# The state and diagonal products of one unit in four move a pair later, beside the transposes of the unit that follows a pair of B and C

## The chip, the cores and the metric

The kernel runs on one core of one Trainium2 chip. The metric is the device time of one execution in microseconds (us), as the median of three runs, 1308.15 us before the change (1307.92 to 1314.77). TensorE (PE) multiplies, VectorE (DVE) and ScalarE (ACT) work on what it leaves in PSUM, GpSimd (POOL) and SyncE (SP) issue transfers between HBM and SBUF.

## The reference

One layer of a Mamba-2 mixer over 512 positions and 2048 channels, with an RMSNorm ahead and one behind. Cut to what matters here:

```python
hn = rmsnorm(x, ln_g)                      # 512 x 2048
z, xbc, dt = split(hn @ w_in)              # 4096 | 4096 + 8*128 (B) + 8*128 (C) | 64
xbc = silu(causal_depthwise_conv(xbc, conv_w, conv_b))       # 4 taps
xs, B, C = split(xbc)                      # 64 heads of 64 channels, 8 groups of B and C
# per head, in chunks, with decay exp(cumsum(A*dt)) between positions:
y_diag = (C B^T * decay) @ (xs * dt)       # inside a chunk
y_off  = (C @ state) * exp(cs)             # what the state of earlier chunks brings
y = (y_diag + y_off + d_skip * xs) * silu(z)
out = rmsnorm(x + rmsnorm(y, norm_g) @ w_out, final_g)
```

## The kernel before, in words

All matrices are split into a rounded part (hi) and a remainder (lo); a product of two such pairs is three matmuls of 128x128 by 128x256. ACT writes hi (L87), DVE subtracts to get lo (L88). The channels of x and z are cut into 32 **units** of 128 channels (two heads each), the groups of B and C into 8 pairs of tiles. The order of the work is a list: B0 C0, then x and z of units 0 and 1, then B1 C1, unit 2, 3, 4, 5, then B2 C2, unit 6, 7, 8, 9, then B3 C3, and so on: a **pair of B and C** stands between units 4g+1 and 4g+2. The first four entries are computed plainly (the ramp, steps 0 to 127). Each later entry (`pair`, 36 of them) takes its two tiles together by a scheme of seven products (`product`, L629) in place of eight, called R11, T1, R22, T2, R21, T3 and T4; their weights are sums of pieces of `w_in` that are loaded, added and split.

**Steps.** A pair is 28 steps (QS) of six matmuls each, a plain tile 16. Everything that isn't a product of the projection is an event at a step (`add`, `run`): before the matmuls of a step PE, SP and POOL issue the events of that step. The orders of PE, SP and POOL are written by hand in this way; on DVE and ACT a scheduler sets the order when the program is built, with what stands under `urgent` preferred. All queues are in order, so an instruction that waits holds what is behind it.

**A unit's own work.** After product T3 of its pair, DVE adds the parts of x (L687 reads the PSUM tile `R`, L691 the tile `S`, both write the tile `xr`), scales them (L693) and runs the convolution (`conv_silu`, L388 and three times L391), and ACT applies SiLU (L394, tile `xs`). z follows a few steps later (`gate`, L643 and L644). Then, at steps counted from the unit's own start, in the table `steps` (six numbers: load, decay, transposes, state, diagonal product, end):

- load, 42: SP loads the tile `csb` (L440) and `ecs` (L443).
- decay, 54 (`u_decay`): twelve ACT instructions of 128x128 (L456, L457, L458), one exponential (L459) and a multiply on DVE (L461) fill the tile `m`. `m`, like `csb`, `xd` and `xw`, has one buffer.
- transposes, 44 (`u_xt`, L473): PE transposes `xs`, DVE makes `xd` (L476) and `xw` (L479).
- state, 72 (`u_state`, L488): PE multiplies `Bt` and `xw`; ACT and DVE split the result (L403, L404).
- diagonal product, 72 (`u_yd`, L502, L506): PE multiplies `xd` and `m`; DVE adds it to `xs` (L509).
- end, 78 (`u_yo`, L518 to L520): C times the state; DVE L521 to L523 form the result `z`, SP writes it to HBM (L524, `yscr`), ACT and DVE sum its squares (L529, L530).

With 28 steps between units, step 72 of one unit is step 44 of the next: the state and diagonal products of unit u stand right ahead of the transposes of unit u+1. Where a pair of B and C stands between, they are apart: unit 5 has its state and diagonal products in unit 6's pair, and the transposes of unit 6 stand alone in unit 7's pair, 28 steps later.

**The ramp.** Units 0, 1 and 31 have rows of their own. At steps 114 to 126 `x_form3` (L575 to L579) rewrites parts of the input through `xr`, one after the other. The last plain tile, C1, is scaled into `xr` (L398) and convolved from there before the first pair may write `xr` at L687.

**The end of the pairs.** The output projection's first weight pieces are loaded by `get_out`: piece 0 into `rc` nine steps, piece 1 into `rb` four steps before the last pair ends. `rb` has one buffer.

## Time and profile before

| | |
|---|---|
| median of three runs | 1308.15 us (1307.92 to 1314.77) |
| the profiled execution's own time | 1305.56 us |
| its span, first to last instruction | 1303.8 us |
| mean granted clock of PE | 0.985 |
| busy share PE, DVE, ACT | 95%, 83%, 65% |
| busy of GpSimd | 77.8 us (6%) |
| moved by DMA | 225.90 MB, mean 173 GB/s |

The span is the time from the first to the last instruction; the run's own time lies 1.8 us above it. Busy time of PE counts pipelined matmuls and is no measure of its peak. A row of a timeline reads: start, length, engine, line, operation, output tile <- input tiles, and in brackets how long the engine was idle before it and what ended that. A row of the waits reads: engine, tile and line that waited, what for, total us, times, longest. A row of the windows reads: stretch, its length, busy us of each engine (instructions), the granted clock as a fraction of full speed, the DMA share.

### The profile page before, as it was taken

The page shows a single profiled execution, that of the slowest core. Times are in us where ns is not written, and L with a number is a line of the kernel's source. Part 1 is how long each engine was busy: PE and PEld are TensorE (multiplying, and loading weights), DVE is VectorE, ACT ScalarE, POOL GpSimd, SP SyncE. Part 2 cuts the span into 40 slices and gives each one's busy share as a digit, 9 for nine tenths or more (in the row PEclk, how much of TensorE's full clock was granted, in tenths as well). Part 3 has the DMA queues.
Part 4 walks back from the last instruction along what each step waited for, and adds up shares of the span by engine and source line. Part 5 has one row for each costly group of instructions (what it writes and reads, how often), then busy time and mean ns, then how long its engine had stood idle before and what let it go on. Part 6 is the DMA issues. An engine that isn't in the chain of part 4 may idle for free.

```text
span 1303.8 us, 24525 instructions
## 1 busy us (share of the span) xinstructions
PE 1243.5 (95%) x9932; PEld 1185.1 (91%) x9932; DVE 1081.8 (83%) x1449; ACT 847.0 (65%) x1371; POOL 77.8 (6%) x99
## 2 busy tenths in 40 slices
PE   8989899989989999999999999999999999999897
PEld 8979799989989998998999899899978899899885
DVE  5796889978989998898989789898856987877765
ACT  7667677667768767776786777678666445434433
POOL 0000000000000000000000000010000000000000
PEclk9999999999999999999999999999999999999999
DMA  9546756666667667667675666666437676657612
GB/s 358 184 132 175 182 149 163 177 162 193 164 164 191 160 170 171 194 153 190 177 179 154 183 168 163 190 169 184 138 105 230 190 198 204 189 125 217 184 57 97
DMA packets 70194, 225.90 MB, mean 173 GB/s; under 512 B 8384, under 2 KB 12800, under 8 KB 69952
## 3 DMA queue, kind: packets, MB, share of 16 engines
q1 hardware_dynamic: 56688, 176.34, 38.6%
q0 software_dynamic: 12672, 46.14, 22.4%
q8 instruction: 78, 1.28, 0.4%
q10 hardware_dynamic: 720, 1.84, 0.4%
q14 instruction: 36, 0.29, 0.1%
HBM read 211.52 MB, written 12.78 MB: 172 GB/s over the span
## 4 chain that ended last, share of the span: by engine, by line
PE 59%; DVE 16%; DMA 11%; ACT 7%; issue 6%; SPq 0%; DVEq 0%; ACTq 0%
PE S L636 4%; PE S L638 4%; PE S L637 4%; PE R L636 4%; PE R L637 4%; PE R L638 4%; DMA csb<-cscr 3%; DVE lo L88 3%; PE mm L636 3%; PE mm L637 3%; PE mm L638 3%; PE mm L932 3%; PE mm L934 3%; PE mm L933 3%; ACT hi L87 3%
## 5 line engine op out<-in xcount | busy, mean ns | idle before, releaser
L88 DVE TENSOR_TENSOR lo<-ra,hi 128x1024 fp32r<-128x1024 f32 x150 | 183.3, 1222 | 48.2 <-ACT hi L87 48.0
L87 ACT CAST hi<-ra 128x1024 fp32r<-128x1024 f32 x150 | 157.0, 1049 | 95.8 <-PE S L637 30.0
L636 PE MATMUL R<-s,hi 128*128 128x256 f32 x576 | 166.9, 290 | 2.3 <-DVE xr L687 2.3
L638 PE MATMUL R<-s,lo 128*128 128x256 f32 x576 | 162.4, 282 | 0.9 <-DVE lo L88 0.9
L637 PE MATMUL R<-s,hi 128*128 128x256 f32 x576 | 162.5, 282 | 0.0
L638 PE MATMUL mm<-xh,lo 128*128 128x256 f32 x576 | 159.4, 277 | 1.5 <-DVE lo L88 1.5
L636 PE MATMUL mm<-xh,hi 128*128 128x256 f32 x576 | 159.3, 277 | 0.0
L637 PE MATMUL mm<-xl,hi 128*128 128x256 f32 x576 | 159.2, 276 | 0.0
L87 ACT CAST hi<-rc 128x1024 fp32r<-128x1024 f32 x94 | 99.0, 1054 | 89.8 <-PE R L637 36.0
L88 DVE TENSOR_TENSOR lo<-rc,hi 128x1024 fp32r<-128x1024 f32 x94 | 115.1, 1225 | 35.2 <-ACT hi L87 35.0
L636 PEld LDWEIGHTS R<-s,hi 128*128 128x128 f32 x576 | 111.9, 194 | 3.6 <-DVE xr L687 2.5
L638 PEld LDWEIGHTS R<-s,lo 128*128 128x128 f32 x576 | 111.4, 193 | 1.1 <-DVE lo L88 1.1
L637 PEld LDWEIGHTS R<-s,hi 128*128 128x128 f32 x576 | 111.7, 194 | 0.0
L638 PEld LDWEIGHTS mm<-xh,lo 128*128 128x128 f32 x576 | 108.3, 188 | 1.9 <-DVE lo L88 1.9
L636 PEld LDWEIGHTS mm<-xh,hi 128*128 128x128 f32 x576 | 108.1, 188 | 0.3 <-issue 0.2
L637 PEld LDWEIGHTS mm<-xl,hi 128*128 128x128 f32 x576 | 108.1, 188 | 0.0
L605 DVE TENSOR_TENSOR ra<-ra,rc 128x1024 f32<-128x1024 f32 x88 | 107.5, 1222 | 0.4
L636 PE MATMUL S<-xh,h1h 128*128 128x256 f32 x288 | 79.7, 277 | 0.0
L638 PE MATMUL S<-s,lo 128*128 128x256 f32 x288 | 79.7, 277 | 0.0
L637 PE MATMUL S<-xl,h1h 128*128 128x256 f32 x288 | 79.6, 277 | 0.0
L638 PE MATMUL S<-xh,h1l 128*128 128x256 f32 x288 | 79.6, 277 | 0.0
L636 PE MATMUL S<-s,hi 128*128 128x256 f32 x288 | 79.6, 276 | 0.0
(448 smaller groups left out, 3958.1 us busy)
## 6 DMA issues: line engine op xcount, KB each, us to landing
rc<-in_wi SPq DMA_DIRECT2D x76, 512.0 KB, 5.1
ra<-in_wi SPq DMA_DIRECT2D x42, 512.0 KB, 6.0
rb<-in_wi SPq DMA_DIRECT2D x40, 512.0 KB, 4.6
ra<-in_wi POOLq DMA_DIRECT2D x36, 512.0 KB, 6.2
rb<-in_wi POOLq DMA_DIRECT2D x36, 512.0 KB, 6.2
csb<-cscr SPq DMA_DIRECT2D x32, 512.0 KB, 5.4
ra<-in_wo SPq DMA_DIRECT2D x26, 512.0 KB, 5.2
yscr<-z SPq DMA_DIRECT2D x32, 256.0 KB, 4.4
```

The costliest lines, as they stand in the source:

```text
L87: S.copy(out=hi, in_=raw)
L88: V.tensor_tensor(out=lo, in0=raw, in1=hi, op=ALU.subtract)
L605: V.tensor_tensor(out=raw, in0=raw, in1=qs[n][other], op=ALU.add)
L636: T.matmul(ps, hi[:, k, :], ah, start=first and k == 0, stop=False, skip_group_check=True)
L637: T.matmul(ps, hi[:, k, :], al, start=False, stop=False, skip_group_check=True)
L638: T.matmul(ps, lo[:, k, :], ah, start=False, stop=k == KH - 1, skip_group_check=True)
L932: T.matmul(ps, yh, hi, start=first and k == 0, stop=False)
L933: T.matmul(ps, yh, lo, start=False, stop=False)
L934: T.matmul(ps, yl, hi, start=False, stop=last and k == 1)
```

## The change

Three things are changed. In the table, units 5, 9, 13, 17, 21 and 25 (the units ahead of a pair of B and C) have state and diagonal product at step 100 in place of 72 and the end at 106 in place of 78: one pair later, in the same step as the transposes of the next unit and ahead of them. Units 0 and 1 get the same pattern: state and diagonal product of unit 0 stand ahead of unit 1's transposes (step 136 of the whole), those of unit 1 ahead of unit 2's (step 172). In the first pair the sum of x is formed in place in the tile `sn`, which holds the copies, and only the scaling (L693) writes `xr`. And the load of the second output piece is issued three steps earlier than its split.

```diff
+    def out_load(n, name):
+        oraw[n] = load_piece(wo_src(*wo_order[n]), OSH, name)
...
     def get_out(n, name="ra"):
         if n < len(wo_order) and n not in opieces:
-            opieces[n] = split_piece(load_piece(wo_src(*wo_order[n]), OSH, name), OSH,
+            raw = oraw.pop(n) if n in oraw else load_piece(wo_src(*wo_order[n]), OSH, name)
+            opieces[n] = split_piece(raw, OSH,
                                      *((op, ("oh", "ol")) if n % 4 == 3 else (wp,)))
...
         sn = sp.tile([P, 2, LH], F32, name="sn")
-        zq = xr[:, 3:L + 3]
+        zq = sn.rearrange("p h l -> p (h l)") if n == 0 else xr[:, 3:L + 3]
...
-        V.scalar_tensor_tensor(out=zq, in0=zq, scalar=-1.0, in1=rbc, op0=ALU.mult, op1=ALU.mult)
+        V.scalar_tensor_tensor(out=xr[:, 3:L + 3], in0=zq, scalar=-1.0, in1=rbc, op0=ALU.mult, op1=ALU.mult)
...
-    steps = {0: [66, 71, 63, 75, 87, 92], 1: [56, 65, 50, 68, 86, 92], NU - 1: [36, 46, 44, 65, 65, 71]}
+    steps = {0: [66, 71, 63, 104, 104, 114], 1: [56, 76, 72, 108, 108, 114], NU - 1: [36, 46, 44, 65, 65, 71]}
+    for u in range(5, NU - 4, UPG):
+        steps[u] = [42, 54, 44, 100, 100, 106]
...
-    add(END - 4, get_out, 1, "rb")
+    add(END - 7, out_load, 1, "rb")
+    add(END - 4, get_out, 1)
```

How this moves instructions is read from the order of the built program. Line numbers of the changed file are 6 higher from L165 to L716 (L394 becomes L400) and 8 or 9 higher behind that.

ACT, from unit 6's pair into unit 7's, before: `m<-csb` is unit 6's decay, `xs<-xs` its SiLU.

```order
L87 CAST h1h<-ra 128x1024
L660 COPY mm<-S 128x256
L456 ACTIVATE m<-csb,cs 128x128
L457 ACTIVATE m<-csb,cs 128x128
L458 ACT_TABLE_LOAD
L458 ACTIVATE m<-csb,nwl 128x128
L665 COPY sn<-R 128x256
L87 CAST hi<-rc 128x1024
L456 ACTIVATE m<-csb,cs 128x128
L394 ACT_TABLE_LOAD
L394 ACTIVATE xs<-xs 128x512
L644 ACTIVATE z<-z 128x512
```

The same place after the change; `stsh` is now the split of unit 5's state:

```order
L87 CAST h1h<-ra 128x1024
L666 COPY mm<-S 128x256
L87 CAST hi<-rc 128x1024
L671 COPY sn<-R 128x256
L400 ACTIVATE xs<-xs 128x512
L87 CAST hi<-rc 128x1024
L650 ACTIVATE z<-z 128x512
L87 CAST hi<-rb 128x1024
L688 COPY sn<-S 128x256
L409 CAST stsh<-yo 128x128
L462 ACTIVATE m<-csb,cs 128x128
```

The decay moved from ahead of the SiLU to behind it, and a table load went. `m` is read by the diagonal product of unit 5, which now stands in this pair too.

SP, in the pairs of units 6 and 7, before: `yscr` is unit 5's result, the `csb` and `ecs` behind it are unit 6's.

```order
L81 DMA rc<-in_wi 128x1024
L81 DMA rb<-in_wi 128x1024
L524 DMA yscr_101<-z 128x512
L440 DMA csb<-cscr 128x1024
L443 DMA ecs<-escr 64x256 x2
L81 DMA rc<-in_wi 128x1024
L81 DMA ra<-in_wi 128x1024
L81 DMA rc<-in_wi 128x1024
L81 DMA rb<-in_wi 128x1024
L440 DMA csb<-cscr 128x1024
```

After:

```order
L81 DMA rc<-in_wi 128x1024
L81 DMA rb<-in_wi 128x1024
L446 DMA csb<-cscr 128x1024
L449 DMA ecs<-escr 64x256 x2
L81 DMA rc<-in_wi 128x1024
L81 DMA ra<-in_wi 128x1024
L81 DMA rc<-in_wi 128x1024
L81 DMA rb<-in_wi 128x1024
L530 DMA yscr_101<-z 128x512
L446 DMA csb<-cscr 128x1024
```

The write of unit 5's result moved from ahead of unit 6's `csb` to ahead of unit 7's.

DVE, in the first pair and the one behind it, before: L687 and L691 form the first pair's sum, `bc` is the convolution of C1.

```order
L398 TENSOR_TENSOR xr<-S,rbc 128x512
L88 TENSOR_TENSOR lo<-ra,hi 128x1024
L388 TENSOR_SCALAR bc<-xr,par 128x512
L605 TENSOR_TENSOR ra<-ra,rc 128x1024
L391 SCALAR_TENSOR_TENSOR bc<-xr,par,bc 128x512
L521 TENSOR_TENSOR ecs<-yo,ecs 128x256
L391 SCALAR_TENSOR_TENSOR bc<-xr,par,bc 128x512
L522 TENSOR_TENSOR xs<-xs,ecs 128x256
L391 SCALAR_TENSOR_TENSOR bc<-xr,par,bc 128x512
L523 TENSOR_TENSOR z<-xs,z 128x512
L687 TENSOR_TENSOR xr<-R,sn 128x256
L691 TENSOR_TENSOR xr<-S,sn 128x256
```

After; `m` is unit 1's, `lo<-rb` the split of the first pair's T3, L583 and L585 belong to the last `x_form3`:

```order
L467 TENSOR_TENSOR m<-m,cbm 128x1536
L693 TENSOR_TENSOR sn<-R,sn 128x256
L582 TENSOR_TENSOR xr<-xr,xl 128x512
L88 TENSOR_TENSOR lo<-rb,hi 128x1024
L583 TENSOR_TENSOR xr<-xr,xl 128x512
L529 TENSOR_TENSOR z<-xs,z 128x512
L88 TENSOR_TENSOR lo<-ra,hi 128x1024
L585 TENSOR_TENSOR xl<-xr,xh 128x2x256
L88 TENSOR_TENSOR lo<-ra,hi 128x1024
L697 TENSOR_TENSOR sn<-S,sn 128x256
L404 TENSOR_TENSOR xr<-S,rbc 128x512
```

The first pair's sum moved from behind C1's convolution to ahead of C1's scaling (L398, now L404), and the split of T3 and the last `x_form3` now stand behind its first half.

## Prediction

> **What bounds the kernel now.** First the head of the page and its chain, then the waits of PE:

> ```profile
> span 1303.8 us, 24525 instructions
> PE 1243.5 (95%) x9932; PEld 1185.1 (91%) x9932; DVE 1081.8 (83%) x1449; ACT 847.0 (65%) x1371; POOL 77.8 (6%) x99
> PE 59%; DVE 16%; DMA 11%; ACT 7%; issue 6%; SPq 0%; DVEq 0%; ACTq 0%
> ```

> ```profile
> PE tr L473 <- ACT xs L394: 22.4, 7, 4.4
> PE mm L932 <- DVE z L643: 2.8, 1, 2.8
> PE R L636 <- DVE xr L687: 2.3, 1, 2.3
> PE mm L638 <- DVE lo L88: 1.5, 2, 1.2
> PE R L638 <- DVE lo L88: 0.9, 1, 0.9
> ```

> PE is the bound, and time is to be had only where it waits or its clock is lowered. The largest wait comes seven times: the transposes (L473) wait for a SiLU (L394). There are 32 units; the seven are units 2, 6, 10, 14, 18, 22 and 26, those behind a pair of B and C. The timelines of DVE, SP, ACT and PE at unit 6 show why:

> ```profile
> 259.96 0.69 DVE L523 TENSOR_TENSOR z<-xs,z 128x512 f32<-128x512 f32 x1
> 260.68 0.33 SPq L524 DMA_DIRECT2D yscr<-z  x1
> 261.05 0.46 SPq L440 DMA_DIRECT2D csb<-cscr  x1
> 266.75 1.54 DVE L391 SCALAR_TENSOR_TENSOR xs<-xr,par,xs 128x512 f32<-128x512 f32 x2
> 268.95 0.41 ACT L456 ACTIVATE m<-csb,cs 128x128 f32<-128x128 f32 x1 [5.38 <-DMA csb<-cscr]
> 272.89 1.28 ACT L394 ACT_TABLE_LOAD   x1
> 274.18 0.63 ACT L394 ACTIVATE xs<-xs 128x512 f32<-128x512 f32 x1
> 274.86 1.12 PE L473 MATMUL tr<-ident,xs 128*128 128x128 f32 x4 [4.38 <-ACT xs L394]
> ```

> The convolution is done at 268.29, but the SiLU starts only at 274.18: ahead of it in ACT's queue stands the decay's first instruction, which waits for `csb` until 268.95; `csb` was held on SP behind unit 5's `yscr`, which waited for `z`. In an ordinary pair the decay can't be put there, because `m` has one buffer and the preceding unit's diagonal product reads it in the same step. The windows of six periods (five pairs each, from one unit's end to that of the fourth after) give the price; the first, the last and the sum of the six:

> ```profile
> core 0: us, PE busy (x) PEld busy (x) DVE busy (x) ACT busy (x) POOL busy (x), PEclk, DMA share, GB/s
> 188.21:303.03 114.82, 110.44 (x960) 107.81 (x959) 99.61 (x128) 81.95 (x139) 8.60 (x10) 0.99 0.64 170
> 753.60:865.20 111.60, 108.40 (x960) 105.78 (x959) 99.51 (x128) 81.53 (x138) 8.57 (x10) 1.00 0.65 174
> sum 676.99, PE 657.20 PEld 641.47 DVE 597.32 ACT 490.61 POOL 51.63; mean PE 109.53 PEld 106.91 DVE 99.55 ACT 81.77 POOL 8.60
> ```

> PE idles 676.99 - 657.20 = 19.8 us in them. The same 960 instructions take 108.40 us busy in the last, at clock 1.00, and 110.44 in the first, at 0.99 in the mean: 657.20 - 6 x 108.40 = 6.8 us more.

> **The change part by part.**

> *Units 5 to 25.* No instruction of PE or DVE is added. The state and diagonal products go into the next unit's pair, ahead of the transposes that waited. Three things follow. First, the decay of unit 6 must now wait until unit 5's diagonal product has read `m`, so ACT has it behind the SiLU, as in ordinary pairs. Second, `csb` loses its place behind `yscr` on SP; `yscr` now stands ahead of unit 7's `csb`, where an ordinary pair has it. Third, DVE's work on unit 5 (L404, L509, L521 to L523, L530) leaves a stretch in which DVE had no idle time and enters one where it idled. Three stretches show that cover, an ordinary pair, the one that ends unit 5's work, and the stretch with unit 7's pair behind the wait:

> ```profile
> 211.64:233.52 21.88, 21.88 (x197) 21.30 (x196) 20.03 (x26) 18.02 (x32) 1.71 (x2) 1.00 0.70 186
> 233.52:255.02 21.50, 21.50 (x193) 20.92 (x192) 21.29 (x28) 13.51 (x24) 1.74 (x2) 1.00 0.60 155
> 276.00:303.03 27.03, 27.03 (x228) 26.45 (x228) 22.39 (x27) 21.38 (x38) 1.72 (x2) 0.97 0.70 200
> ```

> DVE was busy 21.29 of 21.50 us in the second and 22.39 of 27.03 in the third. The ordinary pair runs its 21.88 us without any PE wait with DVE busy 20.03, and unit 7's pair becomes such a pair. PE reached the transposes at 274.86 - 4.38 = 270.48; the SiLU can start once the convolution ends at 268.29 at the latest and takes 0.63, so it is done by 269 with nothing ahead of it, and the products moved in front give PE more work before it asks. I take the whole 19.8 + 6.8 = **26.6 us**. From below: if DVE, at 99.5 of 108.4 us, puts back 1 us per period, 20.6. More than 26.6 there is not, since 108.40 is PE's own work.

> The second part of that sum is the clock. Windows right behind a wait: two in the ramp, one at unit 10, one at the end:

> ```profile
> 147.61:151.30 3.69, 3.69 (x19) 3.69 (x20) 3.69 (x6) 1.95 (x5) 0.19 (x1) 0.56 0.86 218
> 161.50:165.20 3.70, 3.70 (x21) 3.70 (x20) 0.77 (x2) 2.35 (x6) 0.00 (x0) 0.54 0.61 214
> 388.70:392.40 3.70, 3.70 (x33) 3.70 (x34) 2.26 (x3) 3.68 (x6) 0.00 (x0) 1.00 0.78 281
> 947.17:951.00 3.83, 3.83 (x11) 3.08 (x12) 1.08 (x1) 2.17 (x5) 0.00 (x0) 0.61 0.96 278
> ```

> Behind most waits, that of 2.3 us included (at 147.61), PE is granted little more than half its clock for about 3.5 us and does 19 to 21 matmuls where 33 fit. [...]

> *The ramp.* Four waits can go: 2.3 (L687), the first unit's share of the seven, 22.4 - 19.8 = 2.6, and 1.2 and 0.9 for splits. Behind the first two lie the clock windows at 147.61 and 161.50; 3.7 us at a clock of 0.55 lose about 1.6 each. Together 7.0 + 3.2 = 10.2. The first pair's wait goes since its sum no longer stands behind C1's convolution:

> ```profile
> 145.86 0.75 DVE L391 SCALAR_TENSOR_TENSOR bc<-xr,par,bc 128x512 f32<-128x512 f32 x1
> 147.13 0.43 DVE L687 TENSOR_TENSOR xr<-R,sn 128x256 f32<-128x256 f32 x1
> 147.46 0.42 DVE L691 TENSOR_TENSOR xr<-S,sn 128x256 f32<-128x256 f32 x1
> 140.55 0.69 DVE L398 TENSOR_TENSOR xr<-S,rbc 128x512 f32<-128x512 f32 x1
> ```

> New waits come in. The second pair's R11 takes the PSUM buffer of C1, which is free only after L398, and that now stands behind L691, which waits for the end of T3: PE waits 0.42 + 0.69, about 1.2 us with the handover. T3's own lo split stands behind unit 1's decay multiply, L687 and an `x_form3` row, and the last `x_form3`, which T3 reads, behind more splits; splits of 1024 columns take 1.23 (L88, below) and rows of 512 columns 0.69 (L398), so two or three rows too late are 1 to 2.5 us, an estimate. Unit 2's transposes may wait about 1 us, its last tap (L391) being behind the split of unit 1's state. That takes back some 3 to 5 of 10.2. I take **5 us** net; ends 10.2 (no new wait) and -2 (7 us of new waits, and the clock lowered behind three of them at 1.6 each).

> *The output piece.* At the end of the pairs:

> ```profile
> 929.74 1.22 DVE L88 TENSOR_TENSOR lo<-rb,hi 128x1024 fp32r<-128x1024 f32 x1
> 936.86 0.37 SPq L81 DMA_DIRECT2D rb<-in_wo  x1
> 942.75 1.05 ACT L87 CAST hi<-rb 128x1024 fp32r<-128x1024 f32 x1 [3.36 <-DMA rb<-in_wo]
> 943.84 1.23 DVE L88 TENSOR_TENSOR lo<-rb,hi 128x1024 fp32r<-128x1024 f32 x1 [1.73 <-ACT hi L87]
> 946.43 0.68 DVE L643 TENSOR_TENSOR z<-mm,rbc 128x512 f32<-128x512 f32 x1
> 947.17 0.80 PE L932 MATMUL mm<-hi,h1h 128*128 128x512 f32 x1 [2.82 <-DVE z L643]
> ```

> The load was issued at 936.86 behind `yscr`; moved ahead of it, it needs only `rb`, free when L88 ends at 930.96, so it lands some 5.9 us earlier (942.75 - 936.86 = 5.9 from issue), near 937. DVE's 1.73 of waiting goes, and the split, now ahead of the convolution, costs what it cost. So L643 comes 1.7 earlier, and PE's 2.82 shrinks to 1.1; with a smaller wait the low clock behind it (0.61 over 3.83 us, 1.5 us) goes: **3.2 us**. Ends: 1.5 (the clock stays low) and 4.3 (no wait is left).

> Sum: 26.6 + 5 + 3.2 = 34.8. The profiled execution took 1305.56, so 1270.8; the median of the three runs lies 2.6 above it, so **1273**.

> **The rivals.**

> *A new bound in the period.* DVE is at 92% of 108.4, and DMA would move the same bytes in less time. If waits for splits fill half of what is freed, 26.6 becomes 13, the ramp 2 and the end 2: 1291. For it: DVE's 21.29 of 21.50 in the pair of B and C. Against it: the ordinary pairs run at 20.03 of 21.88 without a wait, with a DMA share of 0.70.

> *Slower: T3's split ahead of unit 5's state.* In unit 7's pair ACT now has `hi<-rb` (the weights of T3, whose sum GpSimd fetches) ahead of `sn<-S` and `stsh`; if that transfer is late, the copy, the state, the decay and the SiLU's successors all wait, at six places. GpSimd's row of that transfer and the split before:

> ```profile
> 259.80 0.86 POOL L599 DMA_DIRECT2D rb<-in_wi  x1 [14.18 <-DMA rb<-in_wi]
> 276.73 1.05 ACT L87 CAST hi<-rb 128x1024 fp32r<-128x1024 f32 x1
> rb<-in_wi POOLq DMA_DIRECT2D x36, 512.0 KB, 6.2
> ```

> It lands near 259.80 + 6.2 = 266.0, before PE's 270.48. It makes the kernel slower by 0.5% when it costs (34.8 + 6.5) / 6 = 7 us at each place, that is, from a landing at 277.5: 1315. Eleven us of delay have no source in the trace.

> *The change doesn't do what it says.* If the SiLU has another late input, the seven waits stay, and the end alone gains: about 1305. Against it: 268.29 is the last input's time.

> **How the numbers follow.** About 0.5%, 6.5 us, is what a measurement can tell from no change. The forecast has 0.80 (its own range 1267 to 1281: 41.1 with every term at its upper end, 20.6 + 5 + 1.5 = 27.1 with the first and the last at their lower), the new bound 0.12 (1282 to 1296), no change 0.04, slower 0.04. For 8 in 10 the range goes from 1267 to 1287, into the second case. Faster 0.92, within 0.5% 0.04, slower 0.04.

> **What would show it.** In the changed profile PE's wait for `xs` (L400) is gone or under 2 us in all; each period of four units takes 108.4 to 109.5 us at clock 1.00; ACT no longer waits for `csb` in the periods; PE starts the ramp's L473 of unit 2 without a low clock behind it, and has instead a wait of about 1.2 us of `S` for `xr` (L404); PE's wait for L649 near the end is under 1 us. The prediction is wrong if the periods stay above 110.5, or if PE waits for `lo` (L88) several us in them.

## The result, and the profile after

The changed kernel takes 1274.83 us (median of six runs, 1270.53 to 1279.47) where the kernel before, timed beside it, takes 1308.88 (1307.92 to 1314.77). The ratio is 0.9728 with a 95% interval of 0.9700 to 0.9757, that is, 35.6 us less (31.8 to 39.3); the ratio is worked out from all the runs, the two medians lie 34.05 apart. The forecast was 1273, from a sum of 34.8.

In the changed kernel the line numbers around the units' work are 6 higher: the transposes are L479, the SiLU is L400, the decay L462 to L464, the gate of z L649. The head of its page, and one of PE's waits:

```profile
span 1272.2 us, 24491 instructions
PE 1233.7 (97%) x9932; PEld 1176.2 (92%) x9932; DVE 1079.9 (85%) x1449; ACT 827.5 (65%) x1357; POOL 77.5 (6%) x99
```

```profile
PE tr L479 <- ACT xs L400: 3.4, 8, 1.3
```

The wait of the transposes went from 22.4 us in seven pieces to 3.4 in eight. ACT has 19.5 us less busy time (847.0 before) in 14 instructions fewer: with the SiLU and the decay no longer mixed, it changes its table 71 times in place of 85, and a change takes 1.28 us. The six periods of four units, the first and the sum:

```profile
184.77:293.12 108.35, 108.18 (x960) 105.67 (x959) 99.19 (x128) 78.21 (x134) 8.58 (x10) 1.00 0.69 180
...
sum 651.98, PE 650.30 PEld 634.95 DVE 595.23 ACT 474.32 POOL 51.52; mean PE 108.38 PEld 105.83 DVE 99.20 ACT 79.05 POOL 8.59
```

They take 25.0 us less than the 676.99 of before, and PE's busy time in them, 108.4 us in the mean, goes with a granted clock of 1.00 (108.40 at 1.00 in the last period of before). At unit 6 the timelines of SP, DVE, ACT and PE now read (the first row is the end product of unit 4, a point from which both kernels can be compared):

```profile
230.08 0.28 PE L524 MATMUL yo<-csth,stsh 128*128 128x256 f32 x1
250.79 0.42 SPq L446 DMA_DIRECT2D csb<-cscr  x1
260.29 1.54 DVE L397 SCALAR_TENSOR_TENSOR xs<-xr,par,xs 128x512 f32<-128x512 f32 x2
261.86 0.64 ACT L400 ACTIVATE xs<-xs 128x512 f32<-128x512 f32 x1 [1.43 <-DVE xs L397]
266.41 0.66 PE L479 MATMUL tr<-ident,xs 128*128 128x128 f32 x4
266.53 0.40 ACT L462 ACTIVATE m<-csb,cs 128x128 f32<-128x128 f32 x1 [0.49 <-PE yd L512]
276.39 0.33 SPq L530 DMA_DIRECT2D yscr<-z  x1
```

The SiLU is done at 262.50, PE comes at 266.41: the SiLU, which was 4.38 us late, is 3.91 early. ACT has the decay behind it, started by the end of the diagonal product (`yd`), and `csb` was issued 26 us ahead of `yscr`, so that its transfer is no longer waited for.

The ramp and the end have new waits. The rows are PE's, in the order of time, and one of ACT:

```profile
138.23 0.39 PE L644 MATMUL S<-xh,lo 128*128 128x256 f32 x1 [2.18 <-DVE lo L88]
143.51 0.38 PE L642 MATMUL S<-xh,h1h 128*128 128x256 f32 x1 [0.90 <-ACT mm L698]
158.30 0.66 PE L479 MATMUL tr<-ident,xs 128*128 128x128 f32 x4 [1.31 <-ACT xs L400]
288.53 0.66 PE L479 MATMUL tr<-ident,xs 128*128 128x128 f32 x4 [0.17 <-ACT xs L400]
895.38 1.34 ACT L750 ACTIVATE h1h<-ra,par 128x512 fp32r<-128x512 f32 x2 [5.30 <-DMA ra<-yscr]
900.87 0.66 PE L479 MATMUL tr<-ident,xs 128*128 128x128 f32 x4 [1.11 <-ACT xs L400]
918.96 0.50 PE L941 MATMUL mm<-hi,h1h 128*128 128x512 f32 x1 [1.13 <-DVE z L649]
```

The first is T3's split in the first pair, the second the first product of the second pair, the third unit 2. The fourth comes at six places (units 7, 11, ..., 27), 0.17 each. The last but one, at unit 30, is the same disease at another place: an instruction of ACT that waits 5.30 us for a transfer stands ahead of that unit's SiLU.

Three windows of both kernels show where the rest of the time went: from the first transposes to the end product of unit 2 (the ramp), and from the end of the six periods to the end product of unit 31. First the kernel before, then the kernel after:

```profile
92.19:188.21 96.02, 87.93 (x728) 85.17 (x729) 76.01 (x101) 66.50 (x112) 6.30 (x7) 0.96 0.61 164
865.20:975.45 110.25, 107.19 (x822) 98.65 (x820) 88.21 (x115) 79.52 (x141) 4.33 (x5) 0.98 0.52 146
```

```profile
93.48:184.77 91.29, 85.04 (x728) 82.45 (x729) 76.05 (x101) 63.60 (x111) 6.14 (x7) 0.98 0.64 171
836.75:945.86 109.11, 106.46 (x821) 97.92 (x820) 88.28 (x115) 79.83 (x143) 4.31 (x5) 1.00 0.53 147
```

The ramp is 4.7 us shorter, the end of the pairs 1.1. Behind it lies the output projection, 328.40 us before and 326.38 after, whose order hardly changed; over the profiles of all fourteen kernels it takes 325.8 to 331.9. Ahead of the first transposes the kernel after had lost 1.29 us. 25.01 + 4.73 + 1.14 + 2.02 - 1.29 = 31.6, the difference of the spans.

### The profile page after: what moved, and what is told of

Read it like the earlier page. It is cut to its first block, busy times and chain, and to the rows that moved or that the text cites. A ratio compares the mean times of both kernels' runs of the same rounds, so it can differ in the third digit from the quotient of the medians.

```text
span 1272.2 us, 24491 instructions
## 1 busy us (share of the span) xinstructions
PE 1233.7 (97%) x9932; PEld 1176.2 (92%) x9932; DVE 1079.9 (85%) x1449; ACT 827.5 (65%) x1357; POOL 77.5 (6%) x99
## 3 DMA queue, kind: packets, MB, share of 16 engines
q8 instruction: 78, 1.28, 0.4%
## 4 chain that ended last, share of the span: by engine, by line
PE 63%; DVE 18%; ACT 7%; DMA 6%; issue 5%; SPq 0%; DVEq 0%; ACTq 0%
PE S L644 5%; PE S L642 5%; PE S L643 5%; DVE lo L88 4%; PE R L642 4%; PE R L643 4%; PE R L644 4%; PE mm L644 3%; PE mm L643 3%; PE mm L642 3%; PE mm L941 3%; PE mm L943 3%; PE mm L942 3%; PE mm L879 3%; PE mm L880 3%
## 5 line engine op out<-in xcount | busy, mean ns | idle before, releaser
L88 DVE TENSOR_TENSOR lo<-ra,hi 128x1024 fp32r<-128x1024 f32 x150 | 183.2, 1222 | 47.8 <-ACT hi L87 47.4
L87 ACT CAST hi<-ra 128x1024 fp32r<-128x1024 f32 x150 | 156.7, 1046 | 86.4 <-PE mm L880 19.5
L642 PE MATMUL R<-s,hi 128*128 128x256 f32 x576 | 162.6, 282 | 0.0
L87 ACT CAST hi<-rc 128x1024 fp32r<-128x1024 f32 x94 | 98.9, 1053 | 97.6 <-PE mm L643 37.9
L643 PE MATMUL R<-s,hi 128*128 128x256 f32 x576 | 159.3, 277 | 0.0
L644 PE MATMUL R<-s,lo 128*128 128x256 f32 x576 | 159.2, 276 | 0.0
L643 PE MATMUL mm<-xl,hi 128*128 128x256 f32 x576 | 159.2, 276 | 0.0
L88 DVE TENSOR_TENSOR lo<-rc,hi 128x1024 fp32r<-128x1024 f32 x94 | 115.0, 1224 | 4.3 <-ACT hi L87 4.2
L642 PEld LDWEIGHTS R<-s,hi 128*128 128x128 f32 x576 | 108.4, 188 | 0.0
L643 PEld LDWEIGHTS R<-s,hi 128*128 128x128 f32 x576 | 108.3, 188 | 0.0
L644 PEld LDWEIGHTS R<-s,lo 128*128 128x128 f32 x576 | 108.1, 188 | 0.0
L643 PEld LDWEIGHTS mm<-xl,hi 128*128 128x128 f32 x576 | 108.1, 188 | 0.0
L644 PE MATMUL S<-xh,lo 128*128 128x256 f32 x288 | 80.4, 279 | 2.2 <-DVE lo L88 2.2
L643 PE MATMUL S<-xl,hi 128*128 128x256 f32 x288 | 80.4, 279 | 0.0
L642 PE MATMUL S<-xh,hi 128*128 128x256 f32 x288 | 80.3, 279 | 0.0
## 6 DMA issues: line engine op xcount, KB each, us to landing
rc<-in_wi SPq DMA_DIRECT2D x76, 512.0 KB, 5.3
ra<-in_wi SPq DMA_DIRECT2D x42, 512.0 KB, 6.6
rb<-in_wi SPq DMA_DIRECT2D x40, 512.0 KB, 4.6
ra<-in_wi POOLq DMA_DIRECT2D x36, 512.0 KB, 6.2
rb<-in_wi POOLq DMA_DIRECT2D x36, 512.0 KB, 6.1
csb<-cscr SPq DMA_DIRECT2D x32, 512.0 KB, 5.8
ra<-in_wo SPq DMA_DIRECT2D x26, 512.0 KB, 5.1
```

The costliest lines, as they stand in the source:

```text
L87: S.copy(out=hi, in_=raw)
L88: V.tensor_tensor(out=lo, in0=raw, in1=hi, op=ALU.subtract)
L642: T.matmul(ps, hi[:, k, :], ah, start=first and k == 0, stop=False, skip_group_check=True)
L643: T.matmul(ps, hi[:, k, :], al, start=False, stop=False, skip_group_check=True)
L644: T.matmul(ps, lo[:, k, :], ah, start=False, stop=k == KH - 1, skip_group_check=True)
```

## The experiments

Theory: the seven waits come from ACT's order (the decay, which waits for a late `csb`, ahead of the SiLU that the transposes need). Rivals: the gain comes from the cover (the products that PE has in front of the transposes now), from DVE (whose work on unit 5 left the pair of B and C), or from the time at which `csb` lands alone. Twelve kernels were run; each ratio is to the kernel before timed on the same chip, with its 95% interval.

| kernel | median us | ratio |
|---|---|---|
| e1_units | 1280.94 | 0.9773 (0.9751 to 0.9795) |
| e2_ramp | 1311.63 | 1.0004 (0.9986 to 1.0023) |
| e3_sum | 1305.07 | 0.9961 (0.9943 to 0.9978) |
| e4_out | 1307.74 | 0.9984 (0.9967 to 1.0000) |
| e5_load_late | 1302.21 | 0.9945 (0.9926 to 0.9964) |
| e6_load_early | 1301.03 | 0.9937 (0.9916 to 0.9958) |
| e7_behind | 1273.54 | 0.9726 (0.9707 to 0.9746) |
| e8_decay_later | 1277.90 | 0.9756 (0.9731 to 0.9780) |
| e9_order | 1278.91 | 0.9759 (0.9725 to 0.9792) |
| e10_ramp_pin | 1275.08 | 0.9743 (0.9713 to 0.9773) |
| e11_dve6 | 1287.79 | 0.9833 (0.9801 to 0.9866) |
| e12_order_rest | 1271.96 | 0.9720 (0.9691 to 0.9749) |

### The four parts of the change, one at a time

**e1_units**, the kernel before with the units' new rows alone:

```diff
+    for u in range(5, NU - 4, UPG):
+        steps[u] = [42, 54, 44, 100, 100, 106]
```

> The kernel before, with the new step numbers of units 5, 9, ..., 25 alone (ramp, first pair's sum and output piece as before). Theory (ACT's queue: decay ahead of the SiLU that the transposes need): the six waits of the transposes for the SiLU go, the seventh, unit 2's 2.6 us, stays; the sum of six periods falls by about 25 us (676.99 to about 652), and the kernel with it, 1283 to 1285. Rival (a new bound in the period: DVE or splits): the six waits go and others come, gain 13 or less in this kernel, and the gain of the whole change then lies in the ramp and the end.

Measured: 29.7 us less than the 1310.36 beside it (26.9 to 32.6). The sum of its six periods:

```profile
sum 651.65, PE 650.24 PEld 635.06 DVE 595.15 ACT 474.16 POOL 51.70; mean PE 108.37 PEld 105.84 DVE 99.19 ACT 79.03 POOL 8.62
```

It is the 651.98 of the kernel after. So this part holds five sixths of the gain, and the rival of a new bound in the period falls: 99.2 us of DVE in 108.4 put hardly anything back (651.65 - 650.24 = 1.4 us of idle PE in all six).

**e2_ramp**, the new rows of units 0 and 1 alone:

```diff
-    steps = {0: [66, 71, 63, 75, 87, 92], 1: [56, 65, 50, 68, 86, 92], NU - 1: ...
+    steps = {0: [66, 71, 63, 104, 104, 114], 1: [56, 76, 72, 108, 108, 114], NU - 1: ...
```

> The kernel before, with the new step numbers of units 0 and 1 alone. Theory: unit 2's 2.6 us wait for the SiLU and the low clock behind it (1.6) go, some 1 to 2 us come back as a wait for T3's split, since 2.2 was seen in the changed kernel: 1 to 4 us faster. Rival (the ramp's gain is the first pair's sum alone): no change within 1 us.

Measured: no change (1.8 us less to 3.0 more). One of PE's waits, and the ramp:

```profile
PE R L636 <- DVE xr L687: 4.4, 1, 4.4
```

```profile
91.63:188.72 97.09, 87.89 (x728) 85.11 (x729) 76.58 (x101) 62.83 (x108) 6.15 (x7) 0.95 0.61 161
```

Unit 2's wait of 2.57 is gone and a wait of 1.85 for T3's split came, as expected, but the wait for the first pair's sum grew as well, from 2.3 to 4.4. The theory's 1 to 4 us are not seen; this rival, no change, held.

**e3_sum**, the first pair's sum in `sn` alone:

```diff
-        zq = xr[:, 3:L + 3]
+        zq = sn.rearrange("p h l -> p (h l)") if n == 0 else xr[:, 3:L + 3]
...
-        V.scalar_tensor_tensor(out=zq, in0=zq, scalar=-1.0, in1=rbc, ...
+        V.scalar_tensor_tensor(out=xr[:, 3:L + 3], in0=zq, scalar=-1.0, in1=rbc, ...
```

> The kernel before, with the first pair's sum in a tile of its own alone. Theory: PE's wait of 2.3 us for the end of the first pair's sum goes, in its place comes a wait of about 1 us, and the low clock behind it (1.6) goes: 1 to 3 us faster. Rival (the wait only moves to unit 1's transposes, or to the next split): no change within 1 us.

Measured: 5.1 us less (2.9 to 7.5). Its ramp, and two of PE's waits:

```profile
94.09:187.00 92.91, 86.12 (x729) 83.57 (x730) 75.82 (x101) 63.69 (x111) 6.29 (x7) 0.98 0.66 172
```

```profile
PE tr L473 <- ACT xs L394: 20.6, 7, 3.5
PE S L638 <- DVE lo L88: 3.4, 1, 3.4
```

The wait for the sum is gone, unit 2's as well (the seven that are left are the six periods and unit 30), and a new one of 3.4 came. Of these the theory had only the first, and about 1 us for the new wait; the gain is at the upper end of the 1 to 3 us expected or above. In the profile 3.1 us of the ramp are won. The ramp's gain is this edit; the moved rows give nothing alone, and in the kernel after 1.6 us on top of it (92.91 against 91.29 in one profile each), which the timed runs can't confirm.

**e4_out**, the early load of the second output piece alone:

```diff
...
-    add(END - 4, get_out, 1, "rb")
+    add(END - 7, out_load, 1, "rb")
+    add(END - 4, get_out, 1)
```

> The kernel before, with the load of the second output piece moved ahead of unit 30's store alone. Theory: PE's wait of 2.82 near the end falls to about 1.1, no low clock behind it: 2 to 4 us faster. Rival (the tail is set by the last unit's store and its load for the output, so that what PE wins is waited for later): no change within 1 us.

Measured: 2.1 us less, with an interval that touches no change (0 to 4.3). Its end of the pairs and three of PE's waits:

```profile
872.35:979.55 107.20, 105.83 (x822) 97.60 (x820) 88.21 (x115) 79.01 (x141) 4.32 (x5) 1.00 0.53 148
```

```profile
PE mm L938 <- DVE acc L1041: 2.6, 1, 2.6
PE mm L876 <- DVE acc L916: 2.5, 1, 2.5
PE mm L938 <- DVE z L648: 1.1, 1, 1.1
```

As forecast, the wait for z is 1.1 and the end of the pairs 3.05 us shorter. In this profile the output projection behind it has two waits that are smaller before (0.2 and 0.8); the second is as long in e2_ramp, which doesn't touch that part. That is no rule: over the fourteen profiles, which differ in other edits too, the end of the pairs takes 107.7 us in the mean of the seven with the early load and 110.2 in that of the seven without it, the output projection 328.3 and 329.0. By these means some 2.4 us are won there and not given back behind it.

The four ratios multiply to 0.9723: the parts add up to the whole (0.9728).

### Is it ACT's order, csb, or DVE?

**e5_load_late**, the kernel before with `csb` of units 2, 6, ..., 26 loaded four steps later, which makes ACT take the SiLU first:

```diff
+    for u in range(2, NU - 4, UPG):
+        steps[u] = [46, 54, 44, 72, 72, 78]
```

> The kernel before, with no product moved: for units 2, 6, ..., 26 csb is loaded four steps later (step 46 instead of 42), which turns ACT's order round, so that the SiLU of xs stands ahead of the decay. Theory (the order on ACT is all that matters): the seven waits go or shrink to under 1 us each, as ACT still waits for csb, and longer than before, but behind the SiLU; 20 to 30 us faster. Rival (cover: the gain comes from the products that PE got in front of the transposes, or from DVE's work that moved with them): none of these has moved, so no gain, the seven waits stay. Rival (the late csb): csb lands later still, so slower, by up to 7 x 3 us.

Measured: 7.2 us less (4.7 to 9.7), against the 20 to 30 expected. Unit 6 in the timelines of ACT and PE:

```profile
267.62 0.63 ACT L394 ACTIVATE xs<-xs 128x512 f32<-128x512 f32 x1 [0.47 <-DVE xs L391]
268.69 0.60 PE L473 MATMUL tr<-ident,xs 128*128 128x128 f32 x4
275.09 0.40 ACT L456 ACTIVATE m<-csb,cs 128x128 f32<-128x128 f32 x1 [4.95 <-DMA csb<-cscr]
284.59 0.38 PE L636 MATMUL mm<-xh,hi 128*128 128x256 f32 x1 [1.68 <-ACT mm L692]
```

These transposes don't wait any more, as the order theory says, nor do those at the other five places in the periods (unit 2's still wait 1.82 us). But the decay still waits 4.95 us for `csb`, now ahead of the splits and copies of the following pair, and PE pays 16 us later for ACT's copy (L692), 9.7 us in six pieces, with a granted clock of 0.78, 0.70, 0.61 and 0.58 over the next 3.5 us behind four of them. The theory as stated fails: the order alone only moves the wait. How much of the 7.2 us lies in the periods is open, since unit 2's row in the ramp was changed too: the six periods take 678.39 us here, and 676.99, 681.67, 682.89 and 682.02 in the four profiles with their old rows (before, e2_ramp, e3_sum, e4_out).

**e6_load_early**, the kernel before with `csb` loaded ahead of `yscr`:

```diff
+    for u in range(6, NU - 4, UPG):
+        steps[u] = [20, 54, 44, 72, 72, 78]
```

> The kernel before, with no product moved: for units 6, 10, ..., 26 csb is loaded at step 20 instead of 42, ahead of the preceding unit's yscr on SP, and ACT has the decay far ahead of the SiLU. Theory (the SiLU waits for what stands ahead of it on ACT): the decay no longer waits for csb and is done before the convolution ends, so the six waits of PE go, 20 to 30 us faster. Rival (cover, or DVE's load in the pair of B and C): no product and no sum has moved, so no gain; if DVE is the bound there, waits for splits or for m take the place of the SiLU's.

Measured: 8.2 us less (5.5 to 11.0). Unit 6 in the timelines of ACT, DVE and PE:

```profile
253.98 0.40 ACT L456 ACTIVATE m<-csb,cs 128x128 f32<-128x128 f32 x1
263.34 1.75 DVE L461 TENSOR_TENSOR m<-m,cbm 128x1536 f32<-128x1536 f32 x1
269.20 0.74 DVE L391 SCALAR_TENSOR_TENSOR xs<-xr,par,xs 128x512 f32<-128x512 f32 x1
269.98 0.63 ACT L394 ACTIVATE xs<-xs 128x512 f32<-128x512 f32 x1
270.66 0.70 PE L473 MATMUL tr<-ident,xs 128*128 128x128 f32 x4 [2.10 <-ACT xs L394]
```

The decay no longer waits for `csb` here (0.4 to 0.7 us at the other five places), and ACT takes the SiLU the moment the convolution is done. But the decay's multiply (L461, 1.75) now comes ahead of the convolution's last three taps on DVE, and z's multiply (0.68) and a split (1.22) ahead of the last one, with no idle time between; the convolution ends 1.38 us after PE came to the transposes (268.56). The landing alone isn't enough either; the six periods take 674.93 us.

**e9_order** joins both, with no product moved: `csb` early, and a small copy from `xs` into `m`, overwritten by the decay, that keeps the decay behind the SiLU.

```diff
         m = sp.tile([P, 2, 6, P], F32, name="m")
+        if u % UPG == 2 and 2 < u < NU - 4:
+            S.copy(out=m[:, :, :, 0], in_=un[u]["xs"][:, 0:12].rearrange(...))
...
+    for u in range(6, NU - 4, UPG):
+        steps[u] = [20, 54, 44, 72, 72, 78]
```

> The kernel before, with no product moved: for units 6, 10, ..., 26 csb is loaded at step 20, ahead of yscr on SP, and a small copy from xs into m (12 columns, overwritten by the decay) holds the decay behind the SiLU on ACT. Both other order kernels gained only 7 to 8 us: with the SiLU ahead but csb late, PE waited for ACT's copy behind the decay; with csb early but the decay ahead, its multiply (1.75) delayed the convolution on DVE. Theory (ACT's order and csb's landing together are the cause, unit 5's products need not move): the waits of the transposes shrink to under 1 us each, nothing takes their place, 17 to 25 us faster than before. Rival (DVE: without unit 5's 3.2 us of DVE work leaving that stretch, the convolution ends too late): waits of 1.5 to 2.5 us stay at six places, with low clocks, 12 us faster at most.

Measured: 31.5 us less than the 1309.02 beside it (27.2 to 36.0), more than the 17 to 25 expected. The sum of its six periods, and unit 6 on ACT and PE:

```profile
sum 650.66, PE 650.66 PEld 636.06 DVE 596.50 ACT 475.37 POOL 51.52; mean PE 108.44 PEld 106.01 DVE 99.42 ACT 79.23 POOL 8.59
```

```profile
270.34 0.64 ACT L394 ACTIVATE xs<-xs 128x512 f32<-128x512 f32 x1 [0.51 <-DVE xs L391]
271.37 0.60 PE L475 MATMUL tr<-ident,xs 128*128 128x128 f32 x4
271.71 0.40 ACT L458 ACTIVATE m<-csb,cs 128x128 f32<-128x128 f32 x1
```

No wait is left in 650.66 us. So the whole of this part is had without the change's move: the order on ACT and the landing of `csb` together are the cause. The order on ACT also keeps the decay's multiply behind the convolution on DVE, which e6_load_early lacked. Alone, the landing gives about a quarter (8.2 us), the order 7.2 with the ramp's share in it.

**e7_behind**, the kernel after with the products one step later, behind the transposes:

```diff
-        steps[u] = [42, 54, 44, 100, 100, 106]
+        steps[u] = [42, 54, 44, 101, 101, 106]
```

> The kernel after, with the state and diagonal products of units 5, 9, ..., 25 one step later, behind the transposes of the following unit instead of ahead of them; ACT keeps the SiLU ahead of the decay. Theory (ACT's order): no wait of the transposes comes back, since the SiLU at unit 6 was done at 262.5 and PE came to the transposes at 266.4; 1275 within 4 us. Rival (cover: the products in front give the SiLU the time that it needs): waits of 1 us and more come back at six places, with low clocks behind them, 10 us or more slower than the kernel after.

Measured: as fast as the kernel after. At unit 6:

```profile
259.42 0.63 ACT L400 ACTIVATE xs<-xs 128x512 f32<-128x512 f32 x1 [1.43 <-DVE xs L397]
261.99 0.60 PE L479 MATMUL tr<-ident,xs 128*128 128x128 f32 x4
```

PE comes earlier, but the SiLU is still 1.94 us ahead of it, against 3.91 with the products in front: cover that isn't needed. The 10 us or more that the rival expected are not seen.

**e11_dve6**, the kernel after with DVE's load put back into the pair (the first tap of the convolution seven times, same result; `extra` is 6 for units 6, 10, ..., 26 and 0 for the others):

```diff
-        V.tensor_scalar(out=ca, in0=xr[:, 3:L + 3], ...
+        for _ in range(1 + extra):
+            V.tensor_scalar(out=ca, in0=xr[:, 3:L + 3], ...
```

> The kernel after, with the first tap of the convolution of xs computed seven times instead of once for units 6, 10, ..., 26: 6 x 0.55 = 3.3 us of DVE work put back into the pair of B and C, as much as unit 5's rows took out (3.2); the result is the same. Theory (ACT's order and csb): the SiLU was done 3.9 us ahead of PE, so it still comes in time or up to 1 us late; within 6 us of the kernel after. Rival (DVE's 3.2 us were what counted): the waits are back at six places with 1.5 us and more, and the kernel is 10 us or more slower than the kernel after.

Measured: ratio 0.9833, some 13.7 us slower than the kernel after (0.9833 - 0.9728, of 1309). PE at unit 6, and the SiLU that it waited for:

```profile
265.85 0.63 ACT L401 ACTIVATE xs<-xs 128x512 f32<-128x512 f32 x1 [1.81 <-DVE xs L398]
266.53 0.76 PE L480 MATMUL tr<-ident,xs 128*128 128x128 f32 x4 [2.05 <-ACT xs L401]
```

Here the rival's numbers came in. The SiLU moved by 3.91 + 2.05 = 5.96 us against PE, not by the 3.3 of the added rows, since the scheduler now put z's multiply (L650) and two splits of 1.22 us ahead of the last three taps as well. DVE is not what the change cured, as e9_order has DVE's old load and no wait; but its lead there is only 0.39 us (270.98 to 271.37), where the kernel after has 3.91. The move of unit 5's work bought a margin, not time.

### Towards a better version

**e8_decay_later**, the kernel after with unit 1's decay later, against T3's wait in the ramp (`1: [56, 90, 72, 108, 108, 114]` in place of 76):

> The kernel after, with unit 1's decay at step 90 instead of 76, so that DVE has the split of T3's weights, for which PE waited 2.2 us, ahead of the decay's multiply (1.75 us). Theory (DVE's order set that wait): the wait falls under 0.7 us and the low clock behind it goes, 2 to 4 us faster than the kernel after, 1271 to 1273. Rival (the ramp's DVE is full, and another split is late instead): within 1 us of the kernel after.

Measured: no gain, rather a loss (0.9756 against 0.9728; the intervals overlap). T3's wait went, and this came at unit 2:

```profile
157.41 1.28 ACT L400 ACT_TABLE_LOAD   x1
158.71 0.63 ACT L400 ACTIVATE xs<-xs 128x512 f32<-128x512 f32 x1
```

```profile
159.39 0.90 PE L479 MATMUL tr<-ident,xs 128*128 128x128 f32 x3 [4.73 <-ACT xs L400]
```

ACT now has unit 2's decay ahead of its SiLU, the old fault in a new place.

**e10_ramp_pin** adds the small copy of e9_order for unit 2:

> The kernel after, with unit 1's decay at step 90 as before, and unit 2's decay held behind its SiLU by a small copy from xs into m. Unit 1's decay at 90 alone took T3's wait away, but brought a wait of 4.7 us of unit 2's transposes, since ACT had unit 2's decay ahead of the SiLU, as in the kernel before. Theory (the order on ACT, once more): both waits are gone or under 1.5 us, 1 to 4 us faster than the kernel after, 1270 to 1274. Rival (the ramp's DVE is full: what is taken from one wait comes back in another): within 1 us of the kernel after, or slower.

Measured: 0.9743 (0.9713 to 0.9773), no gain. Unit 2 on ACT and PE:

```profile
154.47 0.63 ACT L400 ACTIVATE xs<-xs 128x512 f32<-128x512 f32 x1 [2.97 <-DVE xs L397]
155.15 0.66 PE L481 MATMUL tr<-ident,xs 128*128 128x128 f32 x4 [3.16 <-ACT xs L400]
```

ACT is free and waits 2.97 us for DVE's last tap: the second expectation held, DVE is full there (its rows run from 147.85 to 155.56 with no idle time between), and what one wait gives another takes.

**e12_order_rest** has the ramp, sum and output piece of the kernel after, with e9_order's edits in place of the moved products:

> The kernel after, with the products of units 5 to 25 put back where they stood before, and the order on ACT set instead, as in the kernel before with csb early and the decay held behind the SiLU; ramp, sum and output piece as in the kernel after. Theory (order and csb are the whole of that part): the same time as the kernel after, 1275 within 3 us. Rival (the 3.5 us that the SiLU is earlier in the kernel after are needed, since in the order kernel it was done only 0.4 us before PE asked): waits come back in a part of the six places, 5 to 15 us slower than the kernel after.

Measured: 0.9720 (0.9691 to 0.9749), the same as the kernel after; its six periods take 649.94 us with PE busy throughout. No kernel was measurably faster than it.

## Why the prediction was right

**Units 5 to 25** (26.6 forecast). 25.0 in the profiles, 29.7 (26.9 to 32.6) in the timed runs of e1_units. The profile of before flattered it: e2_ramp, e3_sum and e4_out, which have the same periods, took 681.67, 682.89 and 682.02 us for the six, because the clock stayed high behind only one wait, or none, where in the profile of before it did so behind two (1.00 over the next 3.5 us at 388.70 and at 839.07; the last section shows on what that hangs); in the six periods PE was busy 661.13, 663.02 and 662.34 us in these three and 657.20 in the profile of before. So "more than 26.6 there is not" held for that one profile alone; the timed runs won more. The mechanism held in its first and second point, ACT's order and `csb`'s place, and the experiments add that they must come together. In its third, DVE's relief, it is true that the convolution ends earlier (261.83 - 230.08 = 31.8 us behind unit 4's end product against 268.29 - 233.52 = 34.8), but e9_order shows that nothing of the gain hangs on it. One clause was wrong: "the products moved in front give PE more work before it asks". They were ahead of the transposes before too, only earlier; PE asks 36.3 us behind unit 4's end product now and asked 37.0 behind it before. The six waits of 0.17 in the periods, 1 us in all, were not foreseen.

**The ramp** (5 forecast). 4.7 in the profiles, by a different sum, so that the agreement is luck. Unit 2's wait of 2.6 was to go by the moved rows, but e2_ramp shows these worth nothing alone; the sum's own tile does it (5.1 alone). The 1.2 us wait came as 0.9, but not for L404, which the forecast named: at 143.51, where PE went on, L404 had not ended; ACT's copy L698 had. T3's split cost 2.18, inside the estimate of 1 to 2.5, and the low clock behind it, held out only for the lower end, did come: 0.55 over the next 3.77 us. Unit 2 came as forecast, 1.3 us and a clock of 1.00 over the next 3.5 us.

**The output piece** (3.2). In place and size shown by e4_out's profile (3.05, the wait 1.1), in the timed runs 2.1 (0 to 4.3). In the kernel after only 1.1 of it shows in that stretch, as unit 30's new wait of 1.11, which the forecast missed, lies there too. The 3.2 us by which the profile after is shorter from the end of the periods on are so in part (2.0) the output projection's own variation.

**The total.** 34.8 against 35.6 is nearer than the terms deserve: against the timed runs of the parts the first was 3 us too small and the last 1 too large.

**The criteria.** The six periods take 108.35 to 109.28 us at clock 1.00, ACT's waits for `csb` are gone from them. The wait of the transposes is 3.4, not under 2, of which 2.4 are unit 2 and unit 30; that for z is 1.1, as the sum had it, not under 1. The rival with T3's split in unit 7's pair had no part: no such wait is in the periods.

## What to carry to other kernels

Where an engine's in-order queue has an instruction that waits for a transfer ahead of one that the bound engine needs, look at two things together, the order and the landing: here they gave 31.5 us together, and mending one (7.2 us, 8.2 us) moved the wait to the next thing in that queue, or into another's (ACT's copy in e5_load_late, DVE's convolution in e6_load_early). Ask of each produced tile how long before its use it is ready (here 4.4 late, 0.4 early, 3.9 early): time is won until that is zero, the rest is margin, and a later edit spends it. In a start-up phase with a full engine, a wait taken off is worth only what isn't waited for next (nothing here in e2_ramp and e10_ramp_pin); the parts have to be run alone before their sum is believed.

## What the runs showed of the hardware

```profile
376.18:379.60 3.42, 1.37 (x15) 1.25 (x12) 3.30 (x5) 1.92 (x4) 0.00 (x0) 1.00 0.97 373
379.60:383.01 3.41, 3.41 (x18) 3.41 (x18) 1.13 (x3) 2.15 (x6) 0.00 (x0) 0.50 0.61 201
485.41:488.82 3.41, 2.74 (x28) 2.09 (x26) 3.34 (x6) 2.01 (x4) 0.00 (x0) 1.00 1.01 253
488.82:492.24 3.42, 2.03 (x18) 2.03 (x19) 3.34 (x6) 2.69 (x5) 0.00 (x0) 1.00 0.97 331
492.24:495.65 3.41, 3.41 (x32) 3.41 (x32) 1.76 (x4) 3.41 (x10) 0.09 (x1) 1.00 0.40 147
```

The first wait lies whole in one step, and the next step has half the clock (0.50): 18 matmuls, against 32 in the step at 492.24. The second is cut by the edge at 488.82 into 0.67 and 1.39 us, and no clock is lost. Over all fourteen profiles, in the steps at full clock between 60 and 1000 us: PE idled more than 1.9 us in 73 of them, and all 73 were followed by a step at half clock; it idled less than 1.6 us in 1805, and none was; of the 15 between, 4 were. The two waits in the profile of before that cost no clock, 3.39 and 3.20 us, were cut as well, at 386.96 and at 837.52.

Told by the length of the wait alone, the same looks like chance. In the same profiles and stretch 60 waits of PE lasted 2.0 to 3.6 us; behind 52 of them the mean clock of the next 3.5 us was below 0.9, behind 8 not, 3.39 and 3.56 us among these. Of the 40 waits between 2.0 and 3.0 us 36 were followed by a low clock, of 46 waits of 1.0 to 1.6 us 5.

The 29 runs of the kernel before beside e1_units spread over 10 us, and the longer one took, the lower as a rule its granted clock (0.985 at 1305.16 us, 0.979 at 1315.19; correlation -0.76 over the 29). That the place of the grid makes this difference is argued and not shown, as each kernel has only one trace.

**A change of ACT's table** takes 1.28 us (the row of e8_decay_later above; 1.283 us in the mean of the 85 in the profile of before). Where the SiLU cuts into unit 6's decay there, one stands ahead of the SiLU, at 272.89, and one more behind it, at 277.80; the one at 272.89 is 1.28 of the 4.38 us that unit 6's transposes waited.
